# One layer of a streaming encoder on one core: order of the first value products and FFN rows, one more weight sum, and the last two rows' scaling

## The chip, the cores and the metric

The kernel runs on one core of a Trainium2 chip. The metric is the device time of one execution in microseconds (us). It was run three times: 1457.06, 1457.77 and 1462.72 us, median 1457.77. One execution was recorded by the hardware profiler: it took 1457.37 us, of which the profile's span holds 1455.5. The granted TensorE clock in it was 0.998 of full speed. All numbers called "before" below are from that execution.

## What is computed

The reference is one layer: RMSNorm, one input projection that feeds a gated convolution and a banded attention, a gated merge, an output projection, then RMSNorm and a SwiGLU FFN, and a last RMSNorm. There are 1024 prompt frames and 64 new frames ("sample"); D is 1024, the FFN has 2816 columns, everything is float32.

```python
def mixer(xn, conv_prefix, attn_fn, w_in, w_conv, w_conv_out, w_attn_out, w_out):
    proj = xn @ w_in
    cb, cc, ch, q, k, v, ga, gb = jnp.split(proj, splits, axis=-1)
    cv, conv_state = causal_conv(cc * ch, conv_prefix, w_conv)
    ya = (cb * cv) @ w_conv_out
    o, new_k, new_v = attn_fn(heads(q), heads(k), heads(v))
    yb = o.reshape(B, L, ATT_DIM) @ w_attn_out
    merged = jax.nn.sigmoid(ga) * ya + jax.nn.sigmoid(gb) * yb
    return merged @ w_out, conv_state, new_k, new_v

def swiglu(x, w1, w3, w2):
    return (jax.nn.silu(x @ w1) * (x @ w3)) @ w2
...
        x = x + m
        x = x + swiglu(rmsnorm(x, g_ffn[l]), w_ff1[l], w_ff3[l], w_ff2[l])
    return rmsnorm(x, g_final), ...
```

## The kernel before

**Rows, and how a product is made.** The 1088 frames lie in nine tiles of 128 rows, called row 0 to row 8 here; row 8 holds the 64 new frames. They are taken in the order 8, 0, 1, 4, 2, 5, 3, 6, 7. Every float32 operand is split in two (`split`, L126): ACT rounds it to a high part with a CAST (L128), DVE subtracts it from the source to get the low part (L129). A product is three matmuls: high by high, low by high, and high by low. The large projections are done on 2 x 2 blocks with seven products in place of eight (`STEPS`), so they need sums and differences of blocks; DVE makes those. In the down product the blocks of a weight group are called b11, b12, b21, b22.

**Order.** The kernel is written in one program order and a tile framework puts every instruction on its engine; each engine runs its own list strictly in that order, and waits on semaphores for the others. `tc.issue_after(x)` adds that an instruction must stand behind x. The engines in what follows: PE (matmuls and transposes), DVE and ACT (vector work, ACT also issues DMAs), POOL (GpSimd: some copies and many DMA issues), SP (DMA issues).

**The start (0 to 68 us).** `normed` (L431) normalises a row, `turned1` (L463) transposes it on PE (L471) into PSUM tile `xt`, and `left_half` or `right_half` (L481, L492) split it into the operand `xn`, whose parts are the tiles `xn_97` to `xn_100`. Row 8 is also split once into `xs8` (tile `xs_135`), all 64 frames side by side, and its frames are then split a second time from PSUM into columns 512 to 543 of the four `xn` parts, 32 frames in each half. `v_tile` (L519) makes the value product of a row: for each of eight slices k, three matmuls (L527 to L529) into `pvv`. Here the tile called `low` holds the rounded high part of a weight slice, and `wv_...` the low part. `split_wv` (L421) splits the weight slices when they arrive. A POOL DMA (L496) stores columns to `x_d` for later sums.

**The start of the FFN (718 to 785 us).** `second(i)` (L1308) makes the second half of the output projection for a row, adds the residual, and normalises (`norm_factor`, L177 to L187, then `xg`, L1323). One row later `turned` (L1327) transposes `xg`, and `first_half` or `second_half` (L1345, L1353) split it and form block sums (`two_sums`, L1362). For the last rows the first FFN products (`Aa`, `Ba`, `Ab`, `Da`, L280) are already interleaved on PE. The Silu activation (L1432) begins behind them, with a load of ACT's function table.

**Down product (1216 to 1447 us).** `Down` (L1555) prepares the seven weight forms of one of eleven groups kp. `frames` (L1609) makes the down product of the new frames (`ys`, L1626) from the forms that exist: with a b12 of its own it takes four matmuls of 256 columns for the block (0, 1), without it four of 512 columns (form 1 plus form 5). `prep` makes that b12 for every kp above 1 except 3.

**The end.** When a row's second half of columns is summed, `half_ended` (L1970) takes the sum of squares, `norm_factor` gives the factor, ACT scales one half (L1988) and sends it (L1989), DVE scales the other with the final gains (L1990) and SP sends it. Row 7 comes next to last and row 3 last, with `ends=True`: its squares are taken in two pieces.

Of the kernel before, what the change touches and what calls it, by code (L numbers as in the profile page):

```python
# [8 lines left out]
F32 = mybir.dt.float32  # L9
# [6 lines left out]
P = 128  # L16
D = 1024
# [49 lines left out]
def encoder_kernel(ctx: ExitStack, tc: tile.TileContext, ins, outs):  # L67
# [108 lines left out]

    def norm_factor(pool, ssq, n, nm, more=None):  # L177

        v, s, y, z, r = (
            pool[:, t : t + 1] if isinstance(pool, bass.AP) else pool.tile([P, 1], F32, tag=f"n{t}", name=f"n{t}{nm}")  # L180
            for t in range(5)
        )
        vec.tensor_scalar(v[:n], ssq, 1.0 / D, EPS if more is None else more[:n], op0=ALU.mult, op1=ALU.add)
        act.activation(s[:n], v[:n], AF.Sqrt)
        vec.reciprocal(y[:n], s[:n])
        vec.scalar_tensor_tensor(z[:n], y[:n], v[:n], y[:n], op0=ALU.mult, op1=ALU.mult)
        vec.scalar_tensor_tensor(r[:n], z[:n], -3.0, y[:n], op0=ALU.add, op1=ALU.mult)  # L187
        return r
# [274 lines left out]
    def turned1(i):  # L463
# [8 lines left out]
        if i == 8:  # L472
            mixed.append(split(xs8[:, :, :TS], xs8[:, :, TS:], pt.rearrange("p a b t -> p (a b) t")[:, :, :TS]))
            left_half(pt[:, :, :, :32], 512, 32)
            right_half(pt[:, :, :, 32:TS], 512, 32)
        elif i < 4:
            left_half(pt, i * P, P)
        else:
            right_half(pt, (i - 4) * P, P)

    def left_half(src, c, n):  # L481
        for g in range(2):
            both(xn.t[g, 0], c, n, src[:, g])
        if c == 256:
            place = mspool.tile([P, D], F32, tag="ms", name="kept")
        else:
            a = KEPT[c in (0, 384)]
            place = scr[:, a : a + D]
# [3 lines left out]
    def right_half(src, c, n):  # L492
        for g in range(2):
            both(xn.t[g, 1], c, n, src[:, g])
        for l in range(2):
            nc.gpsimd.dma_start(x21_d[:, l, :, c : c + n], xn.t[0, 1][:, :, l, c : c + n].bitcast(F32))  # L496
# [22 lines left out]
    def v_tile(i):  # L519
        t0, n = TT[i]  # L520
        pv = bank1("BD", f"pvv{i}")[:, 0]
        for k in range(KD):
            if i == 8:
                a, b = xs8[:, k, :TS], xs8[:, k, TS:]
            else:
                a, b = xn.at(0, k, column(i), P), xn.at(1, k, column(i), P)
            mm(pv[:n], a, wv[k][0], start=k == 0, stop=False)  # L527
            mm(pv[:n], b, wv[k][0], start=False, stop=False)
            mm(pv[:n], a, wv[k][1], start=False, stop=k == KD - 1)  # L529
        put_v(slot(VST, D), pv, n, t0 if t0 < TP else TP + CACHE, nc.gpsimd)  # L530
# [755 lines left out]
    if True:  # L1286
# [58 lines left out]
        def first_half(src, c, n):  # L1345
            f = left[c] = wp.tile([P, 2, 4, P], F32, tag="kept", name=f"kept{c}")[:, :, :, :n]
            act.copy(f, src)
            for g in range(2):
                both(ax[g, 0], c, n, src[:, g])

# [43 lines left out]
        for i in ORDER:  # L1394
            late.append((i, second(i)))
            if len(late) > 1 and i != ORDER[-1]:
                turned(*late.pop(0))


# [152 lines left out]
    class Down:  # L1552
# [15 lines left out]
        def prep(self, step):  # L1568
# [27 lines left out]
            else:  # L1596
                split(*self.new(3), b22)
                self.b12 = None
                if self.kp > 1 and self.kp != 3:
                    minus(b12, b22, b11)  # L1600
# [366 lines left out]

    parts, sums_at = {}, [None, None]

    def half_ended(i, d, ends=False):  # L1970
# [10 lines left out]
        if i not in parts:  # L1981
# [3 lines left out]
            return  # L1985
        r = norm_factor(dp, ssq, P, f"y{i}", parts[i])
        e, row = 1 - d, outs["y_prompt"][i * P : (i + 1) * P]
        act.activation(acc[i, e], acc[i, e], AF.Copy, scale=r)  # L1988
        nc.scalar.dma_start(row[:, e * 512 : (e + 1) * 512], acc[i, e])  # L1989
        vec.scalar_tensor_tensor(x, x, r, gfb[:, d * 512 : (d + 1) * 512], op0=ALU.mult, op1=ALU.mult)  # L1990
        nc.sync.dma_start(row[:, d * 512 : (d + 1) * 512], x)

# [139 lines left out]
```

## Time and profile before

| | before |
|---|---|
| profiled execution | 1457.37 us |
| span of its profile | 1455.5 us |
| PE busy | 1440.5 us (99%) |
| PE weight load busy | 1354.1 us (93%) |
| DVE busy | 1033.2 us (71%) |
| ACT busy | 692.9 us (48%) |
| POOL busy | 156.7 us (11%) |

Busy time is the time in which an engine executes at least one instruction; matmuls overlap, so a row of the timeline gives a start, a duration with the pipeline's depth in it, and the count of like instructions behind each other. The pace of matmuls is read from starts. "[0.58 <-DVE xg L1323]" behind a row means that the engine was idle for 0.58 us ahead of it and that this instruction released it. A row of the timeline is: start in us, duration in us, engine, line, operation, output<-inputs, partitions x elements, count.

### The profile page before, as it was taken

The numbers are of one execution on the slowest core, as the hardware profiler recorded it, in microseconds if no ns is written. First come the engines' busy times: TensorE is split into PE (matmuls) and PEld (weight loads), VectorE is DVE, ScalarE is ACT, GpSimd is POOL, SyncE is SP. The second block draws the span as 40 slices with busy tenths as digits, with TensorE's granted clock in tenths as the row PEclk, the third lists the DMA queues.
The fourth block names the chain that finished last, engine by engine and source line by source line (L and its number), as shares of the span: only waits on it lengthen the run. The fifth ranks groups of instructions, "written<-read, shape, count | busy, mean of one in ns | idle before, by whom it ended". The sixth has DMA issues, their size and how long they took to land.

```text
span 1455.5 us, 26278 instructions
## 1 busy us (share of the span) xinstructions
PE 1440.5 (99%) x10083; PEld 1354.1 (93%) x10083; DVE 1033.2 (71%) x1939; ACT 692.9 (48%) x1389; POOL 156.7 (11%) x292
## 2 busy tenths in 40 slices
PE   8999999999999999999999999999999999999997
PEld 6899999999999989998889999999999998888886
DVE  7975475658447777573588887787777788857676
ACT  7654343335357667531355445444444455512233
POOL 1400010000211121111000111111011111000000
PEclk9999999999999999999999999999999999999999
DMA  8687522225778675843432444433344459767685
GB/s 289 182 278 224 183 74 74 65 101 200 244 224 214 173 188 147 301 144 120 151 109 81 155 170 149 160 141 132 136 142 158 164 202 325 247 231 250 212 270 203
DMA packets 156221, 262.48 MB, mean 180 GB/s; under 512 B 18528, under 2 KB 89376, under 8 KB 156096
## 3 DMA queue, kind: packets, MB, share of 16 engines
q1 hardware_dynamic: 132336, 184.33, 40.1%
q0 software_dynamic: 22608, 74.38, 14.3%
q8 instruction: 79, 1.29, 0.4%
q10 hardware_dynamic: 1152, 2.10, 0.4%
q14 instruction: 46, 0.38, 0.1%
HBM read 171.78 MB, written 90.81 MB: 180 GB/s over the span
## 4 chain that ended last, share of the span: by engine, by line
PE 93%; DVE 3%; ACT 1%; DMA 1%; issue 1%; SPq 0%; ACTq 0%; DVEq 0%
PE A L2042 8%; PE Ab L1852 7%; PE Aa L1852 7%; PE D L2042 4%; PE Db L1852 4%; PE Da L1852 4%; PE J L1863 3%; PE g L348 3%; PE g L347 3%; PE g L346 3%; PE Aga L280 2%; PE B L2042 2%; PE wo L1259 2%; PE wo L1261 2%; PE wo L1260 2%; PE t L1061 2%
## 5 line engine op out<-in xcount | busy, mean ns | idle before, releaser
L346 PE MATMUL g<-xn,wp 128*128 128x272 f32 x320 | 93.9, 293 | 0.0
L347 PE MATMUL g<-xn,wp 128*128 128x272 f32 x320 | 93.0, 291 | 0.0
L348 PE MATMUL g<-xn,low 128*128 128x272 f32 x320 | 92.9, 290 | 0.0
L128 ACT CAST ring<-w2r 128x512 fp32r<-128x512 f32 (+1 forms) x78 | 43.0, 587 | 94.5 <-PE A L2042 49.4
L972 DVE CUSTOM_DVE_ANT_0 p<-s,bb 128x640 f32<-128x640 f32 (+5 forms) x72 | 47.6, 662 | 38.5 <-PE s L1015 36.8
L2042 PE MATMUL A<-ring,low 128*128 128x512 f32 (+1 forms) x270 | 72.6, 384 | 0.0
L2042 PE MATMUL A<-ring,ht 128*128 128x512 f32 (+1 forms) x267 | 72.4, 387 | 0.0
L346 PEld LDWEIGHTS g<-xn,wp 128*128 128x128 f32 x320 | 60.3, 188 | 0.6
L347 PEld LDWEIGHTS g<-xn,wp 128*128 128x128 f32 x320 | 60.3, 188 | 0.4
L348 PEld LDWEIGHTS g<-xn,low 128*128 128x128 f32 x320 | 60.2, 188 | 0.4
L2042 PEld LDWEIGHTS A<-ring,low 128*128 128x128 f32 x270 | 50.1, 188 | 10.2
L128 ACT CAST wa<-rawa 128x512 fp32r<-128x512 f32 x46 | 28.4, 622 | 65.3 <-PE Db L1852 20.9
L2042 PEld LDWEIGHTS A<-ring,ht 128*128 128x128 f32 x267 | 49.8, 188 | 10.2
L982 ACT ACTIVATE p<-p,mx 128x640 f32<-128x640 f32 (+5 forms) x72 | 50.8, 706 | 13.9 <-DVE mx L972 13.5
L129 DVE TENSOR_TENSOR ring<-w2r,ring 128x512 fp32r<-128x512 f32 (+1 forms) x78 | 48.6, 646 | 10.3 <-ACT ring L128 10.3
L129 DVE TENSOR_TENSOR pt<-t,pt 128x640 fp32r<-128x640 f32 (+2 forms) x64 | 41.8, 653 | 15.5 <-ACT pt L128 14.7
L1259 PE MATMUL wo<-low,mg 128*128 128x512 f32 x128 | 50.9, 397 | 0.0
L129 DVE TENSOR_TENSOR low<-rawa,wa 128x512 fp32r<-128x512 f32 x46 | 30.8, 687 | 27.6 <-ACT wa L128 27.6
L1261 PE MATMUL wo<-wo,mg 128*128 128x512 f32 x128 | 50.1, 391 | 0.0
L1260 PE MATMUL wo<-low,mg 128*128 128x512 f32 x128 | 49.9, 390 | 0.0
L1463 POOL DMA_DIRECT2D h_d<-hq_early x44 | 23.8, 541 | 228.2 <-DVE hq_early L129 218.3
L2057 DVE TENSOR_TENSOR acc<-A,acc 128x512 f32<-128x512 f32 x51 | 34.6, 685 | 18.8 <-PE A L2042 18.7
(674 smaller groups left out, 4653.2 us busy)
## 6 DMA issues: line engine op xcount, KB each, us to landing
h_d<-hq_early POOLq DMA_DIRECT2D x44, 512.0 KB, 3.4
ht<-h_d SPq DMA_DIRECT2D x77, 256.0 KB, 3.6
low<-h_d SPq DMA_DIRECT2D x77, 256.0 KB, 3.7
h_d<-hq POOLq DMA_DIRECT2D x23, 512.0 KB, 3.3
rawa<-in_w_ff SPq DMA_DIRECT2D x11, 1024.0 KB, 5.3
rawb<-in_w_ff SPq DMA_DIRECT2D x11, 1024.0 KB, 5.4
w2r<-in_w_ff SPq DMA_DIRECT2D x11, 1024.0 KB, 6.3
qd<-q_d SPq DMA_DIRECT2D x32, 272.0 KB, 4.0
```

Of the source, the lines that this page charges most:

```text
L128: a = act.copy(hi, src)
L129: b = vec.tensor_tensor(lo, src, hi.bitcast(F32), op=ALU.subtract)
L346: mm(out, a, first, start=k == 0, stop=False)
L347: mm(out, a, then, start=False, stop=False)
L348: newest[0] = mm(out, b, p, start=False, stop=k == kt - 1).ins
L972: vec.tensor_tensor_reduce(out=s if len(ps.shape) == 2 else s.rearrange("p (a b) -> p a b", a=2), in0=ps, in1=bias if len(ps.shape) == 2 e ...
L982: act.activation(s, s, AF.Exp, bias=mx, scale=-1.0, accum_out=sm)
L1259: mm(ps, x(k, 0), wh, start=f, stop=False)
L1260: mm(ps, x(k, 1), wh, start=False, stop=False)
L1261: mm(ps, x(k, 0), wl, start=False, stop=e)
L1852: mm(t[:, j, :HN], w[:, k, :], x[:, k, l, j * HN : (j + 1) * HN], start=p in (1, 7) and k == 0 and n == 0, stop=k == 3 and n == 2, skip_gr ...
L2042: mm(t[:, c], ht[k][:, j, x], w[:, l, c], start=p in (1, 2, 7) and k == 0 and n == 0, stop=k == len(ks) - 1 and n == 2, skip_group_check=p ...
```

## The change

Four places change.

- **Value products.** For rows 8 and 0, `v_tile` does all eight high-by-high matmuls first, then the eight with the low part of x, then the eight with the low part of the weights; the other rows keep three matmuls per slice. The 32 new columns of `xn` aren't split from PSUM any more: POOL copies them out of `xs8` (`new_columns`), high and low part of four slices in one CAST of 128x256, four of them. Four CASTs of 128x128 leave ACT, four subtractions of 128x128 leave DVE.
- **FFN rows.** In `first_half` the low parts are put behind the newest row's normalisation (`normed2[-1]`), and a Silu of one column is issued at the end of the loop over rows.
- **b12.** It is also made for kp 1.
- **Last rows.** Row 7's scaling and its two stores are handed over as a function, and issued inside `norm_factor` of row 3, behind its first two instructions.

```diff
--- before.py
+++ after.py
@@ -174,14 +174,17 @@
         t0, n = TT[i]
         return x_p[t0 : t0 + n] if t0 < TP else x_s
 
-    def norm_factor(pool, ssq, n, nm, more=None):
+    def norm_factor(pool, ssq, n, nm, more=None, then=None):
 
         v, s, y, z, r = (
             pool[:, t : t + 1] if isinstance(pool, bass.AP) else pool.tile([P, 1], F32, tag=f"n{t}", name=f"n{t}{nm}")
             for t in range(5)
         )
-        vec.tensor_scalar(v[:n], ssq, 1.0 / D, EPS if more is None else more[:n], op0=ALU.mult, op1=ALU.add)
-        act.activation(s[:n], v[:n], AF.Sqrt)
+        a = vec.tensor_scalar(v[:n], ssq, 1.0 / D, EPS if more is None else more[:n], op0=ALU.mult, op1=ALU.add)
+        b = act.activation(s[:n], v[:n], AF.Sqrt)
+        if then:
+            with tc.issue_after(a.ins), tc.issue_after(b.ins):
+                then()
         vec.reciprocal(y[:n], s[:n])
         vec.scalar_tensor_tensor(z[:n], y[:n], v[:n], y[:n], op0=ALU.mult, op1=ALU.mult)
         vec.scalar_tensor_tensor(r[:n], z[:n], -3.0, y[:n], op0=ALU.add, op1=ALU.mult)
@@ -471,16 +474,26 @@
                 nc.tensor.transpose(pt[:, hf, m, :n], xt[:n, c : c + P], ident[:n, :n])
         if i == 8:
             mixed.append(split(xs8[:, :, :TS], xs8[:, :, TS:], pt.rearrange("p a b t -> p (a b) t")[:, :, :TS]))
-            left_half(pt[:, :, :, :32], 512, 32)
-            right_half(pt[:, :, :, 32:TS], 512, 32)
+            new_columns(pt[:, :, :, :32])
         elif i < 4:
             left_half(pt, i * P, P)
         else:
             right_half(pt, (i - 4) * P, P)
 
+    def new_columns(src):
+        parts = xs8.bitcast(F32).rearrange("p k (l h t) -> p k l h t", l=2, h=2)
+        for h in range(2):
+            for g in range(2):
+                pool_e.tensor_copy(xn.t[g, h][:, :, :, 512:HT], parts[:, 4 * g : 4 * g + 4, :, h])
+        kept_half(src, 512, 32)
+        x21_store(512, 32)
+
     def left_half(src, c, n):
         for g in range(2):
             both(xn.t[g, 0], c, n, src[:, g])
+        kept_half(src, c, n)
+
+    def kept_half(src, c, n):
         if c == 256:
             place = mspool.tile([P, D], F32, tag="ms", name="kept")
         else:
@@ -492,6 +505,9 @@
     def right_half(src, c, n):
         for g in range(2):
             both(xn.t[g, 1], c, n, src[:, g])
+        x21_store(c, n)
+
+    def x21_store(c, n):
         for l in range(2):
             nc.gpsimd.dma_start(x21_d[:, l, :, c : c + n], xn.t[0, 1][:, :, l, c : c + n].bitcast(F32))
 
@@ -519,14 +535,15 @@
     def v_tile(i):
         t0, n = TT[i]
         pv = bank1("BD", f"pvv{i}")[:, 0]
-        for k in range(KD):
-            if i == 8:
-                a, b = xs8[:, k, :TS], xs8[:, k, TS:]
-            else:
-                a, b = xn.at(0, k, column(i), P), xn.at(1, k, column(i), P)
-            mm(pv[:n], a, wv[k][0], start=k == 0, stop=False)
-            mm(pv[:n], b, wv[k][0], start=False, stop=False)
-            mm(pv[:n], a, wv[k][1], start=False, stop=k == KD - 1)
+
+        def x(l, k):
+            return xs8[:, k, l * TS : (l + 1) * TS] if i == 8 else xn.at(l, k, column(i), P)
+
+        terms = [(k, l, w) for k in range(KD) for l, w in ((0, 0), (1, 0), (0, 1))]
+        if i in ORDER[:2]:
+            terms.sort(key=lambda t: (t[2], t[1]))
+        for j, (k, l, w) in enumerate(terms):
+            mm(pv[:n], x(l, k), wv[k][w], start=j == 0, stop=j == len(terms) - 1)
         put_v(slot(VST, D), pv, n, t0 if t0 < TP else TP + CACHE, nc.gpsimd)
         if t0 >= TP - CACHE:
             v32 = slot(V32, ATT)
@@ -1346,7 +1363,10 @@
             f = left[c] = wp.tile([P, 2, 4, P], F32, tag="kept", name=f"kept{c}")[:, :, :, :n]
             act.copy(f, src)
             for g in range(2):
-                both(ax[g, 0], c, n, src[:, g])
+                hi, lo = (ax[g, 0][:, :, l, c : c + n] for l in range(2))
+                act.copy(hi, src[:, g])
+                with tc.issue_after(normed2[-1]):
+                    vec.tensor_tensor(lo, src[:, g], hi.bitcast(F32), op=ALU.subtract)
 
         rest, urgent, normed2, last_forms = [], [], [], []
 
@@ -1395,6 +1415,7 @@
             late.append((i, second(i)))
             if len(late) > 1 and i != ORDER[-1]:
                 turned(*late.pop(0))
+        act.activation(some[:, 12:13], some[:, 11:12], AF.Silu)
 
 
     operands = {p: ax[gh] for p, gh in PLAIN.items()} | tt
@@ -1596,7 +1617,7 @@
             else:
                 split(*self.new(3), b22)
                 self.b12 = None
-                if self.kp > 1 and self.kp != 3:
+                if self.kp not in (0, 3):
                     minus(b12, b22, b11)
                     if self.kp in (7, 10):
                         t = early.tile([P, 2, D], F32R, tag="raw", name=f"b12_{self.kp}")
@@ -1965,7 +1986,7 @@
     ys = psD.tile([P, 2, 512], F32, tag="ys", name="ys")
     frames_due = list(blocks[0])
 
-    parts, sums_at = {}, [None, None]
+    parts, sums_at, scaled = {}, [None, None], []
 
     def half_ended(i, d, ends=False):
 
@@ -1983,12 +2004,19 @@
             vec.tensor_scalar(m, ssq, 1.0 / D, EPS, op0=ALU.mult, op1=ALU.add)
             vec.tensor_tensor(x, x, gfb[:, d * 512 : (d + 1) * 512], op=ALU.mult)
             return
-        r = norm_factor(dp, ssq, P, f"y{i}", parts[i])
-        e, row = 1 - d, outs["y_prompt"][i * P : (i + 1) * P]
-        act.activation(acc[i, e], acc[i, e], AF.Copy, scale=r)
-        nc.scalar.dma_start(row[:, e * 512 : (e + 1) * 512], acc[i, e])
-        vec.scalar_tensor_tensor(x, x, r, gfb[:, d * 512 : (d + 1) * 512], op0=ALU.mult, op1=ALU.mult)
-        nc.sync.dma_start(row[:, d * 512 : (d + 1) * 512], x)
+        r = norm_factor(dp, ssq, P, f"y{i}", parts[i], scaled.pop() if ends else None)
+
+        def scale():
+            e, row = 1 - d, outs["y_prompt"][i * P : (i + 1) * P]
+            act.activation(acc[i, e], acc[i, e], AF.Copy, scale=r)
+            nc.scalar.dma_start(row[:, e * 512 : (e + 1) * 512], acc[i, e])
+            vec.scalar_tensor_tensor(x, x, r, gfb[:, d * 512 : (d + 1) * 512], op0=ALU.mult, op1=ALU.mult)
+            nc.sync.dma_start(row[:, d * 512 : (d + 1) * 512], x)
+
+        if i == 7:
+            scaled.append(scale)
+        else:
+            scale()
 
     q = 0
     for b, ks in enumerate(blocks):
```

How the lists of the engines change, at three places. First PE at the start of the program, from its fourth row on. Names: `warm` are matmuls on constants, `pvv_236` is row 8's value product and `pvv_301` row 0's (232 and 297 after), `xt_0` the transposes of row 0. Before:

```order
L565 MATMUL warm<-ident 128x128 x8
L527 MATMUL pvv_236<-low,xs_135 64x512
L471 MATMUL xt_0_222<-ident,scr 128x128 x8
L528 MATMUL pvv_236<-low,xs_135 64x512
L529 MATMUL pvv_236<-wv_0_189,xs_135 64x512
L527 MATMUL pvv_236<-low,xs_135 64x512
L528 MATMUL pvv_236<-low,xs_135 64x512
L527 MATMUL pvv_301<-low,xn_97 128x512
L529 MATMUL pvv_236<-wv_1_192,xs_135 64x512
L527 MATMUL pvv_236<-low,xs_135 64x512
L528 MATMUL pvv_236<-low,xs_135 64x512
L529 MATMUL pvv_236<-wv_2_195,xs_135 64x512
```
After:

```order
L582 MATMUL warm<-ident 128x128 x8
L546 MATMUL pvv_232<-low,xs_135 64x512
L474 MATMUL xt_0_218<-ident,scr 128x128 x4
L546 MATMUL pvv_232<-low,xs_135 64x512
L474 MATMUL xt_0_218<-ident,scr 128x128 x4
L546 MATMUL pvv_232<-low,xs_135 64x512 x2
L546 MATMUL pvv_297<-low,xn_97 128x512 x3
L546 MATMUL pvv_232<-low,xs_135 64x512
L546 MATMUL pvv_297<-low,xn_97 128x512
L546 MATMUL pvv_232<-low,xs_135 64x512 x11
L546 MATMUL pvv_232<-wv_0_185,xs_135 64x512
```
The matmuls with `wv_0`, `wv_1` and so on, which need the low part of a weight slice, stood as every third one of row 8; now they all stand behind row 8's other sixteen, and row 0's first ones have come forward between them.

Second, DVE at the start of the FFN, from the normalisation of row 6 (`xg_6`) on. `mg_7342` and `mg_7343` (7338 and 7339 after) are low parts of row 3, `low<-rawa` the low part of an FFN weight, `x_7` the residual sum of row 7. Before:

```order
L183 TENSOR_SCALAR some<-some 128x1
L185 RECIPROCAL some<-some 128x1
L186 SCALAR_TENSOR_TENSOR some<-some 128x1
L187 SCALAR_TENSOR_TENSOR some<-some 128x1
L129 TENSOR_TENSOR mg_7342<-xt_3_8643,mg_7342 128x4x128
L1323 SCALAR_TENSOR_TENSOR xg_6_8635<-x_6_8605,some,gb_row 128x1024
L129 TENSOR_TENSOR mg_7343<-xt_3_8643,mg_7343 128x4x128
L1277 TENSOR_TENSOR x_7_8658<-wo_7_8661,x_7_8658 128x512
L129 TENSOR_TENSOR low<-rawa_8697,wa_1_8704 128x512
L1362 TENSOR_TENSOR two_sums<-xt_6_8737,kept_8538 128x512
```
After:

```order
L183 TENSOR_SCALAR some<-some 128x1
L188 RECIPROCAL some<-some 128x1
L189 SCALAR_TENSOR_TENSOR some<-some 128x1
L190 SCALAR_TENSOR_TENSOR some<-some 128x1
L1340 SCALAR_TENSOR_TENSOR xg_6_8631<-x_6_8601,some,gb_row 128x1024
L1369 TENSOR_TENSOR mg_7338<-xt_3_8639,mg_7338 128x4x128
L1294 TENSOR_TENSOR x_7_8654<-wo_7_8657,x_7_8654 128x512
L129 TENSOR_TENSOR low<-rawa_8694,wa_1_8701 128x512
L1369 TENSOR_TENSOR mg_7339<-xt_3_8639,mg_7339 128x4x128
L183 TENSOR_SCALAR some<-some 128x1
L1382 TENSOR_TENSOR two_sums<-xt_6_8734,kept_8534 128x512
```
`xg_6` stood behind the first low part of row 3; it now stands ahead of both, and the second low part has also moved behind the weight's.

Third, ACT at the end of the program: `ssq_e` is the last sum of squares of row 3, L184 the square root in `norm_factor`, L1988 and L1989 (L2011 and L2012 after) a row's scaling and the issue of its store. Before:

```order
L184 ACTIVATE n1y_15850<-n0y_15849 128x1
L1975 ACTIVATE ring_13726,ssq_1_15883<-acc_1_14037 128x256
L1978 ACTIVATE ring_13726,ssq_e<-acc_1_14037 128x256
L1988 ACTIVATE acc_1_14036<-acc_1_14036,n4y_15853 128x512
L1989 DMA out_y_prompt<-acc_1_14036 128x512
L184 ACTIVATE n1y_15889<-n0y_15888 128x1
L1988 ACTIVATE acc_0_14032<-acc_0_14032,n4y_15892 128x512
L1989 DMA out_y_prompt<-acc_0_14032 128x512
```
After:

```order
L184 ACTIVATE n1y_15852<-n0y_15851 128x1
L1996 ACTIVATE ring_13723,ssq_1_15881<-acc_1_14039 128x256
L1999 ACTIVATE ring_13723,ssq_e<-acc_1_14039 128x256
L184 ACTIVATE n1y_15887<-n0y_15886 128x1
L2011 ACTIVATE acc_1_14038<-acc_1_14038,n4y_15855 128x512
L2012 DMA out_y_prompt<-acc_1_14038 128x512
L2011 ACTIVATE acc_0_14034<-acc_0_14034,n4y_15890 128x512
L2012 DMA out_y_prompt<-acc_0_14034 128x512
```
The root of row 3 (`n1y_15889`, after `n1y_15887`) stood behind row 7's scaling and its store, and now stands ahead of both. On POOL the four CASTs `xn_97<-xs_135` to `xn_100<-xs_135` of 128x4x2x32 stand ahead of the first two stores to `x_d`; SP's list has not changed.

## The prediction

> **What bounds the kernel now.** I read the page's busy shares first, then the chain that ended last, then the list of what PE waited for.
>
> ```profile
> span 1455.5 us, 26278 instructions
> ...
> PE 93%; DVE 3%; ACT 1%; DMA 1%; issue 1%; SPq 0%; ACTq 0%; DVEq 0%
> ```
>
> ```profile
> PE warm L458 <- ACT ones L456: 2.9, 1, 2.9
> PE t L1061 <- DVE pt L129: 1.1, 5, 0.4
> ...
> PE xt L1334 <- DVE xg L1323: 0.6, 1, 0.6
> ...
> PE Ab L280 <- ACT wb L128: 0.4, 1, 0.4
> ```
>
> ```profile
> 1446.98 0.52 PE L2042 MATMUL A<-ring,low 128*128 128x256 f32 x3
> ```
>
> The chain is PE for 93% of the span, and in the list of PE's waits (total, times, longest) the one of 2.9 lies before the first matmul and no other is above 1.1. The last matmuls (1446.98) end at 1447.5, 8 us before the span does. So an edit can gain only by closing one of these small waits, by taking matmuls away, or by shortening the end; and whatever it takes from PE is gone from the end one for one, since PE runs without a gap behind it. 0.5% of this kernel, about what a measurement of it can tell from no change, is 7.3 us: more than every wait that the four edits touch.
>
> **Part 1, the start.** Rows 8 and 0 get their value products by terms, and GpSimd fills the 32 new columns.
>
> ```profile
> 12.12 0.44 PE L529 MATMUL pvv<-wv,xs 128*64 128x512 f32 x1 [0.15 <-DVE wv L129]
> ...
> 17.94 0.50 PE L528 MATMUL pvv<-low,xn 128*128 128x512 f32 x1
> 18.27 0.39 PE L529 MATMUL pvv<-wv,xn 128*128 128x512 f32 x1
> 18.50 0.39 PE L527 MATMUL pvv<-low,xn 128*128 128x512 f32 x1
> ...
> 19.89 0.60 PE L471 MATMUL xt<-ident,scr 128*128 128x128 f32 x4
> ...
> 24.25 1.06 PE L471 MATMUL xt<-ident,scr 128*128 128x128 f32 x8
> ```
>
> From 12.12 PE is paced by itself, one matmul every 0.23 us (18.27 to 18.50), with one hole ahead of 17.94. It reaches the transposes of row 4 at 24.25; that time is my mark for the start. In the new order all eight hi·hi products of row 8 come first, so PE now runs at the pace at which ACT rounds the eight weight blocks.
>
> ```profile
> 14.35 1.18 ACT L128 CAST low<-wv 128x512 fp32r<-128x512 f32 x2
> 15.40 0.30 ACT L128 CAST xn<-xt 128x128 fp32r<-128x128 f32 x1
> 15.55 1.10 ACT L436 ACTIVATE scr<-scr 128x1024 f32<-128x1024 f32 x1
> ```
>
> The last two weight casts end at 15.53. Four casts of 128x128 leave ACT; each moves the next start by 0.15 (15.40 to 15.55), three of them stand ahead, so the last block is ready at 15.53 - 3 x 0.15 = 15.1. Behind it PE has 37 matmuls of 0.23 and the eight transposes of row 1 at 0.11 (row 4's eight took 1.06, the time in flight of the last one included): 8.5 + 0.9 = 9.4, so 24.4 to 24.5 in place of 24.25. **+0.15 us** from the order alone: the holes before 12.12 and 17.94 close, but PE waits more between 12 and 15.
>
> The rest of this part is decided on DVE. It subtracts the eight low halves of the weights without a gap, and the four GpSimd copies fall into that train.
>
> ```profile
> 11.38 0.68 DVE L129 TENSOR_TENSOR wv<-wv,low 128x512 fp32r<-128x512 f32 x1
> 11.98 0.28 DVE L129 TENSOR_TENSOR xn<-xt,xn 128x128 fp32r<-128x128 f32 x1
> 12.18 1.28 DVE L129 TENSOR_TENSOR wv<-wv,low 128x512 fp32r<-128x512 f32 x2
> ...
> 18.86 1.41 DVE L451 SCALAR_TENSOR_TENSOR scr<-scr 128x512 f32<-128x512 f32 x2
> ```
>
> The copies need only the low half of xs8, which DVE subtracts just ahead of the row at 11.38, so they are due from about 11.5 on. What a GpSimd cast does beside such a subtraction is shown at 662, and what it takes alone at 637:
>
> ```profile
> 661.88 0.68 DVE L129 TENSOR_TENSOR wo<-wor,low 128x512 fp32r<-128x512 f32 x1
> 662.67 0.73 DVE L129 TENSOR_TENSOR mg<-yg,mg 128x544 fp32r<-128x544 f32 x1
> ```
>
> ```profile
> 637.27 0.24 POOL L1219 CAST ms<-yg 128x64 fp32r<-128x64 f32 x1 [5.06 <-DVE yg L1217]
> ...
> 662.02 0.64 POOL L1219 CAST ms<-yg 128x64 fp32r<-128x64 f32 x1 [5.56 <-DVE yg L1217]
> ```
>
> The cast of 128x64 that takes 0.24 alone was in flight for 0.64: it waited until the subtraction of 661.88 let go. And DVE's next instruction, which normally follows 0.60 after a 128x512 subtraction (11.38 to 11.98), came 0.79 after it, just when the cast was over at 662.66. So the two take turns, and each cast costs DVE 0.19. The Trainium skill has this in "SBUF — State Buffer", Who interferes with whom: a DVE instruction with two SBUF inputs and a GpSimd instruction that reads SBUF exclude each other for a whole instruction. The trace agrees (0.19 lost); without that rule the copies would be free and the sum 1456.1, with it the sum is 1457.4.
>
> How long a copy of 128x256 holds DVE no row shows. Bounds: 0.19, if size costs nothing, and 4 x 0.19 = 0.76, if all of it goes by size. I take 0.35, nearer to the lower end, since most of a small instruction's 0.24 is fixed. The Trainium skill ("GPSIMD Engine Reference", 3.1 Elementwise) gives about 1.8 cycles per element for a good loop; an estimate from that page would be 0.38 per copy, and the sum by it 1457.5.
>
> Four copies then hold DVE for 4 x 0.35 = 1.4 us (0.8 to 3.0). Is there cover? Four subtractions of 128x128 leave DVE (0.20 each, 11.98 to 12.18), but reordering puts two short subtractions and a column product that stood behind L451 ahead of it; summed by their spacings, row 1's normalisation (L451 before, L454 now, two halves) starts at 18.9 without copies, as before at 18.86. Its first half releases the transposes of row 1 some 0.7 later, 19.6. PE arrives there 20 matmuls behind 15.1, at 19.7 (before: 19.89). So there is 0.1 us of cover and the rest is a stall: 1.4 - 0.1 = **+1.3 us**. With PE this much later the later uses (row 4's transposes, the low halves of xn) have slack. After that PE is gapless to 68 us, so the shift stays. Part 1: +0.15 + 1.3 = **+1.45** (bounds +0.15 to +3.05). GpSimd's own next work, the two issues of x_d, start behind four turns of about 0.95 (0.60 for DVE and 0.35) from 11.5, so at 15.3; a cast that waits for them stands behind the snapshot copies on ACT, some us later.
>
> **Part 2, the start of the FFN.**
>
> ```profile
> 760.48 0.66 PE L280 MATMUL Aa<-mg,wa 128*128 128x272 f32 x4
> 761.73 1.09 PE L1334 MATMUL xt<-ident,xg 128*128 128x128 f32 x8 [0.58 <-DVE xg L1323]
> ...
> 783.57 0.41 PE L280 MATMUL Aa<-tt,low 128*128 128x272 f32 x2
> 784.40 0.77 PE L280 MATMUL Ab<-tt,wb 128*128 128x272 f32 x4 [0.41 <-ACT wb L128]
> ```
>
> ```profile
> 759.80 0.68 DVE L129 TENSOR_TENSOR mg<-xt,mg 128x512 fp32r<-128x512 f32 x1
> 760.40 1.27 DVE L1323 SCALAR_TENSOR_TENSOR xg<-x,some,gb_row 128x1024 f32<-128x1024 f32 x1
> ...
> 762.79 0.68 DVE L129 TENSOR_TENSOR low<-rawa,wa 128x512 fp32r<-128x512 f32 x1
> ```
>
> By starts, 272-column matmuls follow each other every 0.12, so PE waits 0.75 ahead of 761.73 and 0.58 ahead of 784.40. The normalisation xg of row 6 now goes ahead of the subtraction of 759.80: it starts at about 759.9, 0.1 after that subtraction's start since it needs the factor computed just ahead, not at 760.40, and the transposes at 761.25. PE, with three products Aa ahead of them, is there at 760.85: a wait of 0.40. But the fillers moved too: the Ab products that stood behind the transposes now come six us later, and the next products with low weights need the subtraction of 762.79. It still stands the same three instructions behind xg, so it moves by the same 0.48 to 762.3 and is done at 763.0, while PE, after eight transposes of 0.11 and four products of 0.12 from 761.25, arrives at 762.6: a **new wait of 0.42**. Together 0.82 for 0.75. The gain is at 784: the Silu table is loaded rows earlier, where ACT has idle time, and other products stand where PE waited: -0.68 (0.58, and 0.1 for the first matmul behind a pause, which 17.94 to 18.27 shows too). Part 2: -0.68 + 0.07 = **-0.6** (bounds -1.4, both waits gone, and +0.2).
>
> **Part 3, b12 for step 1 of the down product.**
>
> ```profile
> 1234.70 1.52 PE L1626 MATMUL ys<-ring,ring 128*128 128x512 f32 x6
> ...
> 1236.51 0.62 PE L1626 MATMUL ys<-ring,ring 128*128 128x512 f32 x2
> ...
> 1245.12 2.02 PE L1626 MATMUL ys<-ring,ring 128*128 128x512 f32 x10
> ```
>
> ```profile
> 1234.63 0.69 DVE L129 TENSOR_TENSOR ring<-w2r,ring 128x512 fp32r<-128x512 f32 x1 [1.07 <-ACT ring L128]
> ```
>
> The ten frame matmuls of step 1 run from 1234.70 to 1237.13; those of step 2, which have b12, take 2.02. Four of 512 columns become four of 256: 2.43 - 2.02 = **-0.4**. DVE gains a subtraction and two half-size splits (some 1.3 us, near 1225), ACT two casts; DVE's idle 1.07 at 1234.63 takes most of it before PE needs a ring block. If that cover were gone it would cost up to 1.3 (bounds -0.4 to +0.9).
>
> **Part 4, the end.**
>
> ```profile
> 1448.92 0.75 DVE L1990 SCALAR_TENSOR_TENSOR acc<-acc,n4y,gfb 128x512 f32<-128x512 f32 x1
> 1449.59 0.20 DVE L183 TENSOR_SCALAR n0y<-ssq_e,more 128x1 f32<-128x1 f32 x1
> 1449.67 0.37 ACTq L1989 DMA_DIRECT2D out_y_prompt<-acc  x1
> 1450.09 0.20 ACT L184 ACTIVATE n1y<-n0y 128x1 f32<-128x1 f32 x1 [0.45 <-DVE n0y L183]
> ...
> 1451.72 0.37 ACTq L1989 DMA_DIRECT2D out_y_prompt<-acc  x1
> ```
>
> Row 3's factor stands behind row 7's scaling on DVE (0.67) and its root behind row 7's DMA issue on ACT. Now both go first: the factor at 1449.0, the root at 1449.25, and row 7's scaling fits while DVE waits for the root. Row 7's own scale on ACT, some 0.75 as DVE's, moves back by 0.5 to 1449.45 and its issue to 1450.2; behind that issue (0.37) row 3's scale follows at 1450.6, and the last issue comes at about 1451.3 for 1451.72. Both output rows then stand closer in the DMA queues; the last transfers may gain less than the issue. **-0.45** (bounds -0.8 and 0).
>
> **Sum** against the profiled execution, 1457.37 with 1.87 around the span: +1.45 - 0.6 - 0.4 - 0.45 = 0.0, so **1457.4**; the median shown is 1457.77, 0.4 above, within what the shown runs differ by.
>
> **Rivals.** (a) The copies do not hold DVE, because GpSimd's turn comes only in gaps: start +0.15, time 1456.1. Against it: at 662 the cast got its turn between two DVE instructions. 22%. (b) Slower than before: the copies hold DVE by size, 0.76 each, the point being any lock above 0.35: start +3.05, time 1459.0. For it: strided blocks of 32 columns, of which no row tells. 15%. (c) The change doesn't do what it says at 761 and 784, the waits return behind other instructions: part 2 nought, time 1458.0. 13%. (d) Both FFN waits go, -1.4: 1456.6. 5%. The forecast: 45%.
>
> **The numbers.** The range goes from (a), with some of (d), to (b), with the 0.4 of the runs: 1455.4 to 1459.4. All cases lie within 7.3 us: same 0.97, slower 0.02 for a copy far beyond its bound, faster 0.01.
>
> **What would show it.** Start: the four POOL casts near 11.5 to 15, each of 0.9 in flight, gaps between DVE's weight subtractions, and the transposes of row 4 at 25.8 (24.4 if (a), 27.3 if (b)). FFN: two waits of 0.4 near 761 and 762.6, none at 784. Down: ten frame matmuls in 2.0. End: last ACT issue 0.4 sooner after PE's end. A changed duration anywhere between 70 and 757 would prove me wrong, since nothing is changed there.

## The result, and the profile after

The changed kernel takes 1461.82 us (median of 22 runs, 1459.39 to 1463.69), the kernel before 1457.63 us (22 runs, 1457.05 to 1462.72). The ratio is 1.0026, with a 95% interval of 1.002 to 1.0032: **slower by some 4 us**, less than 0.5%, and outside the range of 1455.4 to 1459.4. Its profiled execution took 1460.06 us with a span of 1458.1, 2.6 more than before; it is the third quickest of the 22, so it shows less than the median loses.

The same PE instructions in both profiles show where the time went.

| PE reaches | before | after | later by |
|---|---|---|---|
| first value product | 10.37 | 10.72 | 0.35 |
| transposes of row 4 (start) | 24.25 | 25.70 | 1.45 |
| first products of the FFN | 760.48 | 761.60 | 1.12 |
| frame matmuls of step 1 | 1234.70 | 1235.41 | 0.71 |
| A products behind them | 1236.96 | 1237.95 | 0.99 |
| the A products 2.7 us on | 1239.68 | 1242.68 | 3.00 |
| end of the last matmul | 1447.50 | 1450.66 | 3.16 |
| span | 1455.5 | 1458.1 | 2.6 |

The list of what PE waited for, in the changed kernel (total, times, longest):

```profile
PE warm L461 <- ACT ones L459: 2.9, 1, 2.9
PE A L2070 <- ACT acc L2083: 1.7, 1, 1.7
...
PE pvv L546 <- ACT low L128: 0.9, 2, 0.6
...
PE A L2070 <- DVE acc L2085: 0.5, 1, 0.5
PE xt L474 <- DVE scr L454: 0.5, 1, 0.5
PE xt L1351 <- DVE xg L1340: 0.2, 1, 0.2
PE rt L1061 <- DVE pt L129: 0.2, 1, 0.2
```

The two waits of the down product, 1.7 and 0.5, were not there before. The wait of 0.5 on L454 is the one forecast at the start. The FFN's two (0.6 on `xg`, 0.4 on `wb`) have shrunk to one of 0.2. Two small differences lie where no engine's list is changed: the kernel before has a wait of 0.2 on L609 at 108 us, which is gone, and the 0.2 on `rt`, at 587 us, is new.

The start, PE's timeline:

```profile
10.72 0.45 PE L546 MATMUL pvv<-low,xs 128*64 128x512 f32 x1 [0.56 <-ACT low L128]
...
20.76 0.66 PE L474 MATMUL xt<-ident,scr 128*128 128x128 f32 x4 [0.50 <-DVE scr L454]
...
25.70 0.63 PE L474 MATMUL xt<-ident,scr 128*128 128x128 f32 x4
```

and DVE's and POOL's rows beside it:

```profile
11.54 5.70 DVE L129 TENSOR_TENSOR wv<-wv,low 128x512 fp32r<-128x512 f32 x8
```

```profile
11.68 3.20 POOL L487 CAST xn<-xs 128x256 fp32r<-128x256 f32 x4 [10.37 <-DVE xs L129]
```

The four copies run between the eight subtractions, one about every 0.8, and the train is longer than eight spacings of 0.60 allow (7 x 0.60 + 0.68 = 4.88). By single instructions, the four spacings with a copy in them are 0.80 or 0.81 and the other three 0.60.

The down product: PE, then ACT, then DVE.

```profile
1235.41 1.09 PE L1647 MATMUL ys<-ring,ring 128*128 128x512 f32 x6
1236.34 0.63 PE L1647 MATMUL ys<-ring 128*128 128x512 f32 x2
1236.81 0.63 PE L1647 MATMUL ys<-ring,ring 128*128 128x512 f32 x2
1237.95 0.97 PE L2070 MATMUL A<-ring,ht 128*128 128x512 f32 x3 [0.52 <-DVE acc L2085]
...
1242.68 0.97 PE L2070 MATMUL A<-ring,ht 128*128 128x512 f32 x3 [1.70 <-ACT acc L2083]
```

```profile
1230.62 0.62 ACT L128 CAST ring<-w2r 128x512 fp32r<-128x512 f32 x1 [1.50 <-DVE w2r L1594]
1234.83 0.62 ACT L128 CAST ring<-w2r 128x512 fp32r<-128x512 f32 x1 [3.59 <-DMA w2r<-in_w_ff]
1235.35 0.62 ACT L128 CAST ring<-sf 128x512 fp32r<-128x512 f32 x1
1235.87 1.14 ACT L128 CAST ring<-w2r 128x512 fp32r<-128x512 f32 x2
1241.53 0.62 ACT L128 CAST ring<-w2r 128x512 fp32r<-128x512 f32 x1 [4.51 <-DVE w2r L1594]
1242.05 1.07 ACT L2083 COPY acc<-A 128x512 f32<-128x512 f32 x2
```

```profile
1236.00 0.69 DVE L129 TENSOR_TENSOR ring<-sf,ring 128x512 fp32r<-128x512 f32 x1 [3.97 <-ACT ring L128]
...
1237.21 1.28 DVE L2085 TENSOR_TENSOR acc<-A,acc 128x512 f32<-128x512 f32 x2
...
1239.61 1.28 DVE L2085 TENSOR_TENSOR acc<-D,acc 128x512 f32<-128x512 f32 x2
1240.81 0.68 DVE L1594 TENSOR_TENSOR w2r<-w2r,sf 128x512 f32<-128x512 f32 x1
```

ACT stands for 3.59 us at a cast that waits for a load from DRAM. Behind it stands the cast `ring<-sf`, whose input DVE had made by 1231.3; DVE is idle for 3.97 because it needs that one. Then both engines are late. DVE's sum out of the PSUM tile A comes at 1237.21, and PE waits 0.52 for it. DVE's `w2r` comes at 1240.81; ACT's next cast waits 4.51 for it, the copies out of A stand behind that cast, and PE waits 1.70 for them. Before, ACT did the casts in another order:

```profile
1229.41 0.62 ACT L128 CAST ring<-sf 128x512 fp32r<-128x512 f32 x1 [2.99 <-DVE sf L1573]
1229.93 0.58 ACT L2055 COPY acc<-D 128x512 f32<-128x512 f32 x1
1230.41 1.14 ACT L128 CAST ring<-w2r 128x512 fp32r<-128x512 f32 x2
1233.98 1.14 ACT L128 CAST ring<-w2r 128x512 fp32r<-128x512 f32 x2 [2.42 <-DMA w2r<-in_w_ff]
```

`ring<-sf` (form 6 of group 2), form 7 and form 5 came first, and only then the cast that waits for group 3's load. The load itself was issued 0.71 later, as late as PE was, and took as long: 8.92 us lie between its issue on SP (1225.06) and its cast before, 9.06 after (1225.77).

The end, ACT in the changed kernel:

```profile
1452.40 0.20 ACT L184 ACTIVATE n1y<-n0y 128x1 f32<-128x1 f32 x1 [0.28 <-DVE n0y L183]
...
1453.24 0.34 ACTq L2012 DMA_DIRECT2D out_y_prompt<-acc  x1
...
1454.41 0.37 ACTq L2012 DMA_DIRECT2D out_y_prompt<-acc  x1
```

The root now stands ahead of row 7's store; the last issue comes 3.75 behind PE's end (before 4.22), and the span ends 7.45 behind it (before 8.0).

### The profile page after: what moved, and what is told of

The parts are those of the page before. It is cut to its first block, busy times and chain, and to the rows that moved or that the text cites. A ratio compares the mean times of both kernels' runs of the same rounds, so it can differ in the third digit from the quotient of the medians.

```text
span 1458.1 us, 26289 instructions
## 1 busy us (share of the span) xinstructions
PE 1441.7 (99%) x10083; PEld 1354.1 (93%) x10083; DVE 1034.2 (71%) x1938; ACT 693.0 (48%) x1388; POOL 159.4 (11%) x296
## 4 chain that ended last, share of the span: by engine, by line
PE 91%; DVE 5%; ACT 2%; DMA 1%; issue 1%; SPq 0%; ACTq 0%; DVEq 0%
PE Aa L1873 7%; PE A L2070 7%; PE Ab L1873 7%; PE Da L1873 4%; PE Db L1873 3%; PE D L2070 3%; PE J L1884 3%; PE pvv L546 3%; PE g L351 3%; PE g L350 3%; PE g L349 3%; PE Aga L283 2%; PE B L2070 2%; PE t L1078 2%; PE Ak L283 2%; PE Aq L283 2%
```

## The experiments

The runs are from three chips; every kernel is compared with runs of the kernel before on its own chip. All of them compute the whole layer.

### Is it b12, and is it the order on ACT?

**The change without b12 for group 1:**

```diff
-                if self.kp not in (0, 3):
+                if self.kp > 1 and self.kp != 3:
```

> The changed kernel with the b12 of group 1 taken back (kp > 1 and not 3, as before); the three other edits stay. In the changed profile PE's row of A matmuls stood 0.71 us later than before at 1235 and 3.12 later at 1243, with new waits of 0.5 and 1.7 on ACT and DVE work in between. Theory H (b12 changed the order on ACT so that a cast that waits for the load of group 3 stands ahead of two casts of group 2): without it these waits go, and the time is 1457.6 + 0.7 - 0.5 = about 1457.8, near the kernel before. Rival S (the loss is the start's, and the waits at 1238 only show work that is late anyway): it stays at 1460 or above. Rival W (b12's own 1.3 us of DVE work costs, not the order): also about 1457.8; the run with another order tells H from W.

**The kernel before with b12 for group 1 alone** (the same line the other way):

> The kernel before with the b12 of group 1 as the only edit. H: PE waits about 2 us more behind the frame matmuls of group 1, gains 0.4 on those, so 1459 to 1461, and the times scatter by some us, since they hang on when a load lands. W: the 1.3 us of DVE work less its cover, at most +0.9: up to 1458.5, without more scatter than before. S: no change or -0.4.

**The whole change with the blocking cast moved.** Group 3's first splits are put behind the cast of group 2's form 7. Of all engines' lists only ACT's differs from the change, by this one cast, which moves behind two others:

```diff
-            if step == 0:
+            if step == 0 and self.kp == 3:
+                with tc.issue_after(seventh_cast[0]):
+                    split(*self.new(1), b11)
+            elif step == 0:
                 split(*self.new(1), b11)
...
-                split(*self.new(7), b11)
+                cast, _ = split(*self.new(7), b11)
+                if self.kp == 2:
+                    seventh_cast.append(cast)
```

(and the same `issue_after` around group 3's split of form 2)

> The whole change, b12 included, with one thing more: the first cast of group 3 on ACT, which waits for that group's load, is put behind the casts of group 2's forms 6 and 7. Nothing else moves on any engine. H: the waits of 0.5 and 1.7 at 1238 to 1243 go, the frame matmuls keep their 0.4: about 1457.4, 0.4 under the run without b12, and little scatter. W: the waits stay with DVE's work, and the time stays at 1460 or above.

**The change itself, once more:**

> The changed kernel itself, once more, so that the runs of this call can be compared with it on one chip. By all theories 1461 to 1462.5, some 4 us above the kernel before, and a scatter of some us.

The last column is how late PE is against the profile before, ahead of this place (at 1234 us) and behind it (at 1246).

| kernel | median, us | runs | ratio to the kernel before, 95% | PE late by, us |
|---|---|---|---|---|
| change without b12 | 1458.13 | 1457.25 to 1459.19 | 1.0003 (0.9994 to 1.0012) | 1.54, 1.54 |
| before, b12 alone | 1460.21 | 1459.16 to 1460.92 | 1.0015 (1.0006 to 1.0023) | 1.17, 3.40 |
| change, cast moved | 1458.15 | 1457.31 to 1460.03 | 1.0003 (0.9994 to 1.0012) | 1.99, 1.58 |
| change again | 1461.43 | 1459.59 to 1464.39 | 1.0027 (1.0018 to 1.0037) | 0.82, 3.82 |
| the change, first profile | 1461.82 | 1459.39 to 1463.69 | 1.0026 (1.002 to 1.0032) | 0.71, 3.15 |

The kernel before ran at 1457.75 beside the first three, at 1457.34 beside the change again (another chip) and at 1457.63 beside the change. Moving one cast takes the ratio from 1.0027 to 1.0003, though b12 and all its DVE and ACT work are still done. PE loses 2.2 to 3.0 us at this place in the three profiles with the new order, nothing without b12, and gains 0.41 with the cast moved. So it is the order, not the work. ACT and PE with the cast moved:

```profile
1232.68 0.62 ACT L128 CAST ring<-sf 128x512 fp32r<-128x512 f32 x1 [0.15 <-DVE sf L1594]
1233.40 0.62 ACT L128 CAST ring<-w2r 128x512 fp32r<-128x512 f32 x1
1236.03 1.15 ACT L128 CAST ring<-w2r 128x512 fp32r<-128x512 f32 x2 [2.00 <-DMA w2r<-in_w_ff]
```

```profile
1236.69 1.09 PE L1659 MATMUL ys<-ring,ring 128*128 128x512 f32 x6
1237.61 0.63 PE L1659 MATMUL ys<-ring 128*128 128x512 f32 x2
1238.08 0.62 PE L1659 MATMUL ys<-ring,ring 128*128 128x512 f32 x2
1238.54 0.85 PE L2082 MATMUL A<-ring,ht 128*128 128x512 f32 x3
```

ACT still waits for the load (2.00), but nothing that PE needs soon stands behind it, and PE goes on without a gap. (Of the 1.99 that PE is late here, 1.04 came between 786 and 850 us, where its matmuls followed each other more slowly without a wait. No other profile shows that, and its cause is open.) The ten frame matmuls take 1.85 (1236.69 to 1238.54), not 2.26 as before (1234.70 to 1236.96): the 0.4 of b12 is real, and too small to show between 1458.13 and 1458.15. b12 alone costs 2.5 us.

That PE's wait hangs on the load is shown by three profiles in which the load landed at different times. First ACT's cast and PE's next A products in the second profile of the change:

```profile
1235.52 0.62 ACT L128 CAST ring<-w2r 128x512 fp32r<-128x512 f32 x1 [4.17 <-DMA w2r<-in_w_ff]
```

```profile
1235.51 1.09 PE L1647 MATMUL ys<-ring,ring 128*128 128x512 f32 x6
...
1238.64 0.97 PE L2070 MATMUL A<-ring,ht 128*128 128x512 f32 x3 [1.10 <-DVE acc L2085]
```

The cast starts 0.01 behind the first frame matmul, and PE's first new wait is 1.10. In the first profile of the change it starts 0.58 ahead, and the wait is 0.52. With b12 alone:

```profile
1235.07 0.62 ACT L128 CAST ring<-w2r 128x512 fp32r<-128x512 f32 x1 [3.42 <-DMA w2r<-in_w_ff]
```

```profile
1235.86 1.09 PE L1626 MATMUL ys<-ring,ring 128*128 128x512 f32 x6
...
1238.20 0.96 PE L2042 MATMUL A<-ring,ht 128*128 128x512 f32 x3 [0.32 <-DVE acc L2057]
```

It starts 0.79 ahead, and the wait is 0.32. In all three the wait is the cast's start, counted from the first frame matmul, plus 1.1: it follows the landing one for one. The second wait is 1.7 in all three. Whether the landing also makes the runs scatter is open: those of the change spread over 4.3 and 4.8 us, but those of b12 alone only over 1.8, where some us had been expected, and the 33 runs of the kernel before beside them over 2.95.

### What the start costs, and why

**The edit of the start alone:**

> The kernel before with only the edit of the start (value products by terms and the GpSimd copies). In the changed profile the transposes of row 4 come at 25.70, not 24.25, and PE is still 1.27 late at 586. If that is the edit's: +1.1 to +1.45, so 1458.7 to 1459.1, and the transposes at about 25.4 to 25.7. If 0.35 to 0.6 of it is only the weights' landing (the first value matmul began 0.35 later in that one execution): +0.6 to +0.9, and they come 0.9 behind a first value matmul's usual time. If the shift is taken up by later waits: no change.

**Only the order of the value products** (the copies as before):

```diff
+        terms = [(k, l, w) for k in range(KD) for l, w in ((0, 0), (1, 0), (0, 1))]
+        if i in ORDER[:2]:
+            terms.sort(key=lambda t: (t[2], t[1]))
```

> The kernel before with only the order of the value products of rows 8 and 0 changed; the 32 new columns are split from PSUM by ACT and DVE as before, GpSimd copies nothing. If the start's cost was the lock of the copies alone: DVE's train as before, no wait ahead of row 1's transposes, time and the transposes of row 4 as before (1457.5, 24.3 behind a first value matmul at 10.4). If the order costs as well, since PE then runs at the pace of ACT's weight casts (0.45 us by the run with late copies: 25.0 - 24.25 - 0.3): transposes of row 4 at 24.7 to 24.9, 1457.9 to 1458.1.

**Only the copies** (the products as before):

```diff
-            left_half(pt[:, :, :, :32], 512, 32)
-            right_half(pt[:, :, :, 32:TS], 512, 32)
+            new_columns(pt[:, :, :, :32])
```

> The kernel before with only the GpSimd copies; the value products keep their order, three matmuls for each weight slice. The four copies hold DVE 0.2 us each in the first half of its train, and the low parts of the weights are now needed every third matmul: PE waits for DVE, so the transposes of row 4 come 0.4 to 0.8 later than 24.25, 1457.9 to 1458.3. If the fewer casts and subtractions outweigh the lock: 24.25 or less, 1457.5.

**The edit of the start, with the copies held until DVE's train is over:**

```diff
+        last = pool_e.tensor_copy(cols[:, 12:13], wv[-1][1][:, :1].bitcast(F32))
+        with tc.issue_after(last.ins):
             for h in range(2):
                 for g in range(2):
                     pool_e.tensor_copy(xn.t[g, h][:, :, :, 512:HT], parts[:, 4 * g : 4 * g + 4, :, h])
```

> The edit of the start alone, as in a4_start, with one GpSimd copy of a single column ahead of the four: it reads the low half of the last weight slice, so the four copies run only when DVE's train of eight subtractions is over. If the copies held DVE (0.2 us each): the train takes 4.9 us, not 5.7, the transposes of row 1 wait 0.6 less, and the time is 0.5 to 0.8 below the edit alone, 1458.5 to 1458.8 beside 1457.7 for the kernel before. If the train's pace has another cause (the casts of ACT): no change, 1459.3. If the later copies make ACT wait for POOL's stores at 23: above 1459.3.

**The same with one copy first and three late:**

```diff
+        first = pool_e.tensor_copy(xn.t[0, 1][:, :, :, 512:HT], parts[:, :4, :, 1])
+        x21_store(512, 32)
+        with tc.issue_after(first.ins):
             last = pool_e.tensor_copy(cols[:, 12:13], wv[-1][1][:, :1].bitcast(F32))
...
-            for h in range(2):
-                for g in range(2):
+            for g, h in ((0, 0), (1, 0), (1, 1)):
```

> The edit of the start with one copy (the part that POOL stores to DRAM) first and the other three behind DVE's train of subtractions. Only POOL's order differs from the edit alone. Against the run with all four late, the store is issued early again, so ACT's cast of the next row into that part does not wait for it; against the edit alone, three locks of 0.2 leave the train. Then the train takes 5.1, and row 4's transposes come 0.5 before those of the edit alone for the same first value matmul: about 25.0, and 1458.5 to 1458.8. If ACT still waits for a store: above 1459.3.

The first value product began anywhere from 10.37 to 11.19 in these profiles, with the landing of the first weights; so the mark is the time from it to the transposes of row 4. One profile gives it only roughly: it is 13.83 to 14.01 in the five profiles whose start is as before, and 14.79 to 15.58 in the five with the whole edit of the start (14.98 in the first profile of the change).

| kernel | median (kernel before), us | ratio, 95% | first product to row 4 | eight subtractions on DVE |
|---|---|---|---|---|
| before | | | 13.88 | with 4 short ones between |
| start alone | 1459.33 (1457.75) | 1.0009 (1.0 to 1.0018) | 15.09 | 5.70 |
| order alone | 1458.84 (1457.45) | 1.0008 (0.9999 to 1.0017) | 14.66 | with 4 short ones between |
| copies alone | 1458.09 (1457.45) | 1.0006 (0.9997 to 1.0015) | not the same order | 5.70 |
| copies late | 1460.08 (1457.34) | 1.0019 (1.001 to 1.0028) | 16.15 | 4.95 |
| one early, three late | 1458.45 (1457.45) | 1.0008 (0.9999 to 1.0017) | 14.19 | 5.33 |

DVE and POOL with late copies:

```profile
11.36 4.95 DVE L129 TENSOR_TENSOR wv<-wv,low 128x512 fp32r<-128x512 f32 x8
```

```profile
16.50 1.44 POOL L490 CAST xn<-xs 128x256 fp32r<-128x256 f32 x4
```

Nothing but POOL's list differs from the edit alone, so the copies lengthen DVE's train: 5.70 - 4.95 = 0.75, **0.19 for each copy**. That is what the cast of 128x64 cost at 662, though this one has four times the columns and takes 0.36 behind the train (1.44 / 4). Yet the time went up:

```profile
26.83 0.63 PE L471 MATMUL xt<-ident,scr 128*128 128x128 f32 x4 [1.81 <-ACT scr L128]
```

```profile
23.76 0.30 ACT L128 CAST xn<-scr 128x128 fp32r<-128x128 f32 x1 [1.59 <-DMA x_d<-xn]
```

ACT's next cast into the part that POOL stores now waits 1.59 for that store, which was issued 3 us later, and PE waits 1.81 behind it. The run with that one copy first removes both: no wait of ACT on the store, and no wait ahead of row 1's transposes. Its mark of 14.19 flatters it: its first product came late, at 11.19, and DVE's train began 0.29 behind it, where it began 0.92 behind with the edit alone; row 4 came at 25.38, for 25.55 there. Its train took 5.33, more than 4.95 + 0.19, because DVE also waited for a cast of ACT: the fifth subtraction starts at 14.31, 0.03 behind the end of ACT's fifth cast of a weight slice. This profile is of the slowest of the eleven runs (1460.62), with a wait of 1.71 at 111 us that no other profile has.

The order alone costs 0.78 in its one profile (14.66 - 13.88), for the reason that the forecast gives, PE at the pace of ACT's casts, but more of it: the widest hole is 0.50, and the four short casts on ACT, which this kernel keeps, stand among the weights'.

```profile
15.16 2.80 PE L530 MATMUL pvv<-low,xs 128*64 128x512 f32 x10 [0.50 <-ACT low L128]
```

With those casts gone and no copies in the train (late copies, less PE's wait of 1.81) 14.34 are left, 0.46 above before. The copies alone show no gain either; that what they take from ACT is given back on DVE, whose train is 5.70 there too, is argued. Of the five forecasts of time, the edit alone came out 0.2 above its range, the order alone 0.7 above, the copies alone came out where they were put, one early, three late at its lower edge, and the late copies as their last case said, through ACT's wait for the store. The intervals of the runs are wide beside such sums (0.0009 is 1.3 us), so the sizes are taken from the profiles; one profile of the edit alone also has 0.7 of waits at 350 (on `Aya`), and kernels without the edit show 0.3 and 0.4 there, so that is not the edit's.

### Is there a version that beats both?

**The FFN rows and the last rows alone, in two calls; and with b12 and the moved cast:**

> Only the edits of the FFN's first rows and of the last rows; the start and b12 as before. By the changed profile the offset fell from 1.27 us (586) to 0.72 (791), and the end is 0.55 shorter behind PE's last matmul: -0.55 - 0.55, so about 1456.6 beside 1457.7 for the kernel before. If the FFN edits only used slack that the late start had given to DVE: -0.5, so 1457.2.

> The edits of the FFN's first rows and of the last rows alone, a second time, on the chip of this call. If their gain is real: 0.6 to 1.1 us below the kernel before again (a ratio of about 0.9994); if the first result was chance: 1.0000 within 0.0003.

> FFN rows, last rows, and b12 for group 1 with the first casts of group 3 held behind group 2's forms 6 and 7; the start as before. If the three add up: -0.55 - 0.55 - 0.4, about 1456.2. If the freed 0.4 us only meets a load that lands when it lands (group 3's): 1456.6, as without b12.

The first gave 1456.68 and 1457.30 us, beside 1457.34 and 1457.52 of the kernel before: ratios 0.9996 (0.9987 to 1.0005) and 0.9997 (0.9988 to 1.0006). With b12 it gave 1457.10, 0.9998 (0.9989 to 1.0007). All three lie below the kernel before and none can be told from it. The profile of the second call has the effects at their places: PE's waits at the FFN's start are one of 0.2 on `xg`, PE's lateness against the kernel before falls from 0.83 at 740 us to 0.38 at 791, and the last store is issued 3.75 us after PE's end, for 4.22 before:

```profile
1447.40 0.52 PE L2056 MATMUL A<-ring,low 128*128 128x256 f32 x3
...
1451.67 0.37 ACTq L1998 DMA_DIRECT2D out_y_prompt<-acc  x1
```

(1451.67 - 1447.92). So about 0.9 us is gained at these places in the profile, and the runs scatter by more than that. The b12 with the cast moved takes 0.41 off PE here as well (0.03 early at 1234, 0.44 at 1246), and the runs don't show it.

## Why the prediction was wrong

**Part 3 failed, and it alone carried the time out of the range** (1458.13 without b12, 1458.15 with the one cast moved). The saving on the frame matmuls was right (0.41 for 0.4). Wrong was the step "DVE's idle 1.07 at 1234.63 takes most of it before PE needs a ring block. If that cover were gone it would cost up to 1.3". It priced b12 by the work that it adds. But the row that it quotes says that DVE was idle because of a cast on ACT, and ACT's cast waited for a load: this was no free room but the end of a chain through a DMA. And the edit moved ACT's list there: the cast that waits for the load went ahead of two that DVE needs. Since an engine's list is strict, these waited for DRAM as well, and PE lost 2.8 us between 1236 and 1243 (an offset of 0.30 after the frame matmuls, 3.12 at 1243). ACT's wait for the load wasn't added; it was moved ahead of work that was ready, and the two lists of ACT, compared at this place, show it. It was not among the rivals, and its cost, 2.6 to 3.4 in three profiles (PE's loss and the 0.41 saved), lies beyond the bound of 1.3.

**Part 1, +1.45: the size came out right by luck, its two terms did not.** In the first profile the transposes of row 4 are 1.45 late, but 0.35 of it is the later landing of the weights. The edit's own is 1.10 there, and 1.27 on average: the mark is 15.16 over the five profiles with this edit and 13.89 over the five without. The order was put at 0.15 and costs more, 0.46 with the short casts gone, by one profile (0.55 to 0.93 if PE's idle time ahead of row 1's transposes is taken off the five marks); the lock was put at 0.35 for each copy and costs 0.19, its lower bound. The mechanism held: turns between DVE and POOL, and a stall ahead of row 1's transposes (0.50 here and 0.35 to 0.79 in the five, forecast 1.3). Rival (a), no lock at all, is refuted by 5.70 against 4.95; rival (b), a lock that grows with size, by 0.19. The Trainium skill ("SBUF — State Buffer", Who interferes with whom) speaks of an exclusive lock. The trace agrees on the turns, but not on a loss as long as the copy: one that takes 0.36 behind the train cost DVE 0.19 in it.

"After that PE is gapless to 68 us, so the shift stays" held to 68 us only. At 108 us the kernel before has its wait of 0.2 on L609, 0.49 by starts, and the changed kernel hasn't, so PE is 0.95 late behind it; at 587 us it loses 0.28 at the new wait on `rt`, and is 1.27 late from there to the FFN. The prediction said that a changed duration between 70 and 757 us would prove it wrong. There are these two, where no list of an engine is changed. The wait on `rt` shows in all seven profiles that have both the new order and the copies, and in no other; why is open.

**Part 2, -0.6: right.** By starts, as the forecast counts, PE waits 0.38 ahead of the transposes at 762.35, for 0.40 (the 0.21 of the row is counted from the end of the matmul before, not from its start); in place of one wait of 0.42 behind them it loses 0.24 between 763.55 and 764.15 and about 0.1 on either side; and the wait at 784 is gone:

```profile
761.60 0.54 PE L283 MATMUL Aa<-mg,wa 128*128 128x272 f32 x3
762.35 0.88 PE L1351 MATMUL xt<-ident,xg 128*128 128x128 f32 x6 [0.21 <-DVE xg L1340]
...
763.55 0.65 PE L283 MATMUL Ba<-mg,wa 128*128 128x272 f32 x3
764.15 0.52 PE L283 MATMUL Aa<-mg,low 128*128 128x272 f32 x2
```

PE's lateness falls from 1.27 ahead of the FFN to 0.72 at 791, by 0.55, and by 0.38 to 0.56 in five further profiles with this edit. Rival (c), waits that come back elsewhere, did not happen, nor did (d): some 0.8 us of waits are left.

**Part 4, -0.45: right** (0.47 by the last issue, 0.55 by the span's end). The span ends 7.45 to 7.54 behind PE in all seven profiles with this edit and 8.02 to 8.10 in the seven without, so the two output rows closer together in the queues cost nothing.

In the first profile, then, the start leaves 1.27, the FFN takes 0.55, the frame matmuls 0.41 and the end 0.55: 0.2 below the kernel before, near the 0.0 of the forecast, had the waits at 1238 to 1243 not come. With their 2.8 it is 2.6, and more in most other runs. The edits measured apart give about the same as the change: 1.6 for the start, 2.5 for b12, and -0.2 and -0.7 for the FFN and the end, in medians, 3.4 to 3.8 beside 4.1 and 4.2.

## What to carry to other kernels

Where a scheduler orders each engine's list, even a small addition can reorder it far from its own instructions: look in every engine's list at the place for instructions that wait for a DMA, and at what they have passed. Idle time that ends with a DMA's landing, also two steps up the chain, is not cover; price such a place by what stands in line behind the load, not by the work added.

## What the runs showed of the hardware

- A GpSimd copy beside DVE's subtractions with both inputs in SBUF costs DVE 0.19 us, for 64 columns (one place, at 662 us) as for 256 (5.70 against 4.95 for four copies), while the copy takes 0.24 and 0.36 where no such subtraction runs.
- The 1 MB load of a weight group takes 8.9 to 9.65 us from its issue to the cast that uses it, in five profiles, while the DMA engines are fully busy (from 1225 to 1235 us their busy share is 1.00 or a little above, and they move 378 to 406 GB/s). In the three profiles with the new order of casts it took 8.89, 9.06 and 9.65, and PE's first wait was 0.32, 0.52 and 1.10.
